# Moving the work beside each attention one stage on: gates beside stick-breaking, the triangular solve beside forgetting attention, the recurrence beside differential attention

## The chip, the cores and the metric

The kernel runs on one core of one Trainium2 chip. The core has a matrix engine (TensorE, PE in the views; its weight loads are listed apart as PEld), VectorE (DVE), ScalarE (ACT), GpSimd (POOL) and SyncE (SP, which issues most transfers). Each engine executes its own instructions in a fixed order; semaphores tie the engines together. The metric is the device time of one execution in microseconds, lower is better.

## The reference

One layer of a hybrid encoder for 1024 prompt tokens and 64 tokens of a second request with 256 cached positions (1088 rows in all, `D_MODEL` 1024). Four branches read one projection of the normalized input, and each has a gate of 1024 columns:

```python
u = rms_norm(x);  proj = u @ w_in          # fox | diff | sb | gdn | gates (4 x 1024)
o_fox  = softmax(q k^T/8 + c_q - c_k) v    # forgetting attention, 4 heads of 64
o_diff = (softmax_1 - lam * softmax_2) v   # differential attention, then a norm
z = q k^T/8                                # stick-breaking attention
o_sb   = exp(log_sigmoid(z) + later) v     # later: reversed cumsum of log_sigmoid(-z)
# gated DeltaNet, chunks of 64 tokens, 4 heads of 64
sol = triangular_solve(I + m, [v*beta, k*beta*exp(g)])   # per chunk and head
for each chunk:
    v_new = u - kc @ S
    o = (q*exp(g)) @ S + a @ v_new
    S = S*exp(g_last) + k'^T @ v_new
merged = sum_i sigmoid(gate_i) * (o_i @ w_branch_i)
x += merged @ w_out;  x += swiglu(rms_norm(x));  y = rms_norm(x)
```

## The kernel before

Matrices are split into a high and a low float16 half, and each product is three matmuls. The program goes through stages, one after the other: norm and transposes; the DeltaNet projection (`gdn_project`); `gdn_pass1`, which works out per chunk the 64x64 matrices m (stored through the dram tile `nd`), decays and scaled keys (`r1d`, `r2d`, `qed`); then the three attentions `attend_sb`, `attend_fox`, `attend_diff`; the merge; the product with `w_out` (tile `pout`); the feed-forward part.

Each attention loops over two pairs of heads and nine query tiles (`QORD`). Per tile TensorE makes scores into `psc`, VectorE and ScalarE turn them into probabilities in `st` (for stick-breaking: `z`, `e` and a reversed scan `cu`), a transposing transfer brings `st` back as `pt`, and TensorE multiplies by the values into `pv` (`po` in the differential attention).

Two lists hold work that is written beside these stages. `dense` is TensorE work: the projections of the three attentions (`project`, tile `pd`, stored to `qd_*`, `kd_*`, `vd_*`) and the gates (`spill_gates`): for each branch, 8 column tiles of 128 and 3 pieces of the 1088 rows, 96 tiles of 24 matmuls into `pgs`, each copied by ScalarE into `ths` and stored to `gtd` by a POOL-issued transfer. `side` is the DeltaNet's serial part: `gdn_solve` (30 steps of the triangular solve on VectorE, tiles `X` and `tmpx`, all chunks and heads at once) and `gdn_seq` (the recurrence over the row tiles t = 8, 0, 1 to 7; two chunks each but for t = 8). A step of `gdn_seq` prepares `py`, `px`, `pu`, `pk`, and then per chunk:

```python
pks = kc @ (Sh, Sl);  vn = u0 - pks;  vh = split(vn)
pds = kd @ vh;  pog = qe @ (Sh, Sl) + aa @ vh
S32 = S1 + pds;  Sh, Sl = split(S32)
```

After its chunks, a row tile gets its norm (`sqo`, `sso`, `ztg`, `osg`) and is stored to `od_gdn`. `fill(us)` takes as much from `dense` as the constants `FILL_SB`, `FILL_FOX`, `FILL_DIFF`, `FILL_GDN` allow, and one piece of `side`. A scheduler then fixes each engine's order from the instructions so written, from their data and from the pools that they need. `drain` writes the rest of a list.

What stands beside what: beside `gdn_pass1` and `attend_sb`, the projections; `gdn_solve` beside `attend_sb` (its first step is held behind `sb_mark`); beside `attend_fox` the recurrence and the gates, which reach through `attend_diff`. The merge takes the branches in the order sb, fox, diff, gdn (tile `ptb`, 96 tiles): its pool `brp`, with `oT` (the branch outputs, transposed) and the branch weights `wbh`, `wbl`, is opened after the recurrence's pool is closed. A gate tile comes back from `gtd` as `thg`; its tanh is on ScalarE, the product and the sum `mg` on VectorE, some sums on POOL.

Of the kernel before, what the change touches and what calls it, by code (L numbers as in the profile page):

```python
# [44 lines left out]

FILL_SB, FILL_FOX, FILL_DIFF, FILL_GDN = 0.0143, 0.006, 0.0155, 8

# [6 lines left out]
def tile_hybrid_encoder(ctx, tc, i, o):  # L54
# [461 lines left out]

    sb_mark = [None]

    def attend_sb():
        for pair in range(2):  # L520
            kT, vt = load_kv("sb", pair)
            for t in QORD:
# [3 lines left out]
                for hp in range(2):  # L526
# [19 lines left out]
                    acopy(sv[:n, 0, :W], z[:n, :W], PS)  # L546
                    sb_mark[0] = stt(sv[:n, 1, :W], z[:n, :W], PS, sv[:n, 0, :W], ALU.mult, ALU.subtract)
                    pts.append(tr())
# [3 lines left out]
    def attend_fox():  # L552
        for pair in range(2):
# [4 lines left out]
            for t in QORD:  # L558
# [3 lines left out]
                for hp in range(2):  # L562
# [15 lines left out]
                    acopy(sv[:n, 0, :W], s[:n, :W], mn[:n, 3:4])  # L578
                    stt(sv[:n, 1, :W], s[:n, :W], mn[:n, 3:4], sv[:n, 0, :W], ALU.mult, ALU.subtract)
                    pts.append(tr())  # L580
# [115 lines left out]
    qed = tc.dram_tile([T, 512], F16, name="qed")  # L696
    nd = tc.dram_tile([18, NH, 64, 64], F32, name="nd")
    xd = tc.dram_tile([17 * NH, 2048], F32, name="xd")
# [5 lines left out]
    def gdn_pass1(g1p, xg):  # L704
# [54 lines left out]
        def scores_of(t, n, gt, rec2):  # L759

            pm = pgd("pm")
            for c in range(1 if t == 8 else 2):
                for h in range(NH):
                    for xy in range(2):
                        pe.matmul(pm[64 * c:64 * c + 64, h * P:(h + 1) * P],
                                  lhsT=gt[:, 2 + xy, h, 64 * c:64 * c + 64],
                                  rhs=gt[:, 0:2, h, 64 * c:64 * c + 64], start=(xy == 0), stop=(xy == 1))
            pm4 = pm.rearrange("p (h v i) -> p h v i", h=NH, v=2)
            dt_t = dT[:, t * NH:(t + 1) * NH]
            a32 = g1p.tile([P, NH, 64], F32, tag="a32", name="a32", bufs=1)  # L770
            n32 = g1p.tile([P, NH, 64], F32, tag="n32", name="n32", bufs=2)
            stt(n32[:n], pm4[:n, :, 1], -(2.0 ** -10), dt_t[:n], ALU.mult, ALU.mult)
            stt(a32[:n], pm4[:n, :, 0], 2.0 ** -5, dt_t[:n], ALU.mult, ALU.mult)
            ra = rec2[:, 1024:].rearrange("p (l h e) -> p l h e", l=2, h=NH)
            acopy(ra[:n, 0], a32[:n])
            tt(ra[:n, 1], a32[:n], ra[:n, 0], ALU.subtract)
            sync.dma_start(r2d[t, 0:n], rec2[:n])
            for c in range(1 if t == 8 else 2):
                gps.dma_start(nd[2 * t + c].rearrange("h j i -> j h i"), n32[64 * c:64 * c + 64])

# [81 lines left out]
    def gdn_solve():  # L862
# [3 lines left out]
        with tc.tile_pool(name="gp2", bufs=1, side="right", reuse_waits="tile") as g2p:  # L866
            X = g2p.tile([NP, 2, 32, 32], F32, name="X")
            tmp = g2p.tile([NP, 512], F32, name="tmpx")
            for q in range(2):
                sl = slice(32 * q, 32 * q + 32)  # L870
                gps.dma_start(X[:, q], nd[0:17, :, sl, sl].rearrange("n h j i -> (n h) j i"))
            for _ in range(3):
                yield 0.0
            for j in range(1, 31):
                r = 31 - j
                behind = tc.issue_after(sb_mark[0].ins) if j == 1 else ExitStack()
                behind.__enter__()
# [18 lines left out]
    def gdn_seq(g3):  # L896
# [30 lines left out]
        for t in [8] + list(range(8)):  # L927
# [11 lines left out]
            for c in range(nch):  # L939
                up, dn = slice(64 * c, 64 * c + 32), slice(64 * c + 32, 64 * c + 64)  # L940
                sync.dma_start(t32[up, :, 0:32], xv[2 * t + c, 0])
                sync.dma_start(t32[dn, :, 32:64], xv[2 * t + c, 1])
                sync.dma_start(t32[up, :, 32:64], nd[2 * t + c, :, 0:32, 32:64].rearrange("h j i -> j h i"))
                sync.dma_start(t11[64 * c:64 * c + 32], xtv[2 * t + c])
# [98 lines left out]

    def spill_gates(b, sp):
        j = bidx[b]
        for d2 in range(4):
            wu = load_unit([(w_in, 0, OFF_GATE + j * D + d2 * BW, BW)], BW)
            for m in range(2):
                d = 2 * d2 + m
                for off, n in PIECES:  # L1050
                    pg = pd("pgs")
                    gemm_a(pg, wu, m * P, uh, ul, off, n, KD)
                    th = sp.tile([P, 364], F32, tag="ths", name="ths", bufs=2)
                    with tc.high_priority():
                        acopy(th[:, :n], pg[:, :n], 0.5 * IWS)
                    gps.dma_start(gtd[b][d * P:(d + 1) * P, off:off + n], th[:, :n])
                    yield 3.7


    with tc.tile_pool(name="gp1", bufs=1, side="right", reuse_waits="tile") as g1p:  # L1060
# [8 lines left out]
        proj = [project(b) for b in ("sb", "fox", "diff")]  # L1069
        dense += proj  # L1070
        for w in gdn_pass1(g1p, xg):
# [7 lines left out]
    with tc.issue_after(pre.ins):  # L1079
        side.append(gdn_solve())  # L1080
        attend_sb()
    drain(dense)
    drain(side)
    pj_.close()
    cb_ = ExitStack()
    cb = cb_.enter_context(tc.tile_pool(name="cb", bufs=1, side="right", reuse_waits="tile"))
    gd_ = ExitStack()
    g3 = gd_.enter_context(tc.tile_pool(name="gp3", bufs=1, side="right", reuse_waits="tile"))
    dense += [spill_gates(b, sp) for b in gtd]
    side.append(gdn_seq(g3))  # L1090
    attend_fox()
    drain(side)
    gd_.close()
    cb_.close()
    br_ = ExitStack()
    brp = br_.enter_context(tc.tile_pool(name="br", bufs=1, side="right", reuse_waits="tile"))
    attend_diff()
    drain(dense)
# [411 lines left out]
```

## Time and profile before

| | |
|---|---|
| time, 3 runs | median 1852.74 us (1850.4 to 1865.82) |
| the profiled execution: own time / span | 1846.53 / 1844.7 us |
| TensorE busy / weight loads busy | 1731.3 us (94%) / 1226.5 us (66%) |
| VectorE / ScalarE / GpSimd busy | 1253.2 / 864.1 / 302.9 us |
| first scores of sb, fox, diff | 301 / 492 / 641 us |
| last gate matmul, first `pout` matmul | 957 / 1065 us |

The stages are told apart by the first matmul of each tile name. Times in the views are microseconds from the start of the span, where not marked ns. A busy share is an average over the whole span; the stretches between these marks have different limits, so the rows below are cut by them.

### The profile page before, as it was taken

To read this page: it belongs to the slowest core of one execution; us is meant where nothing else is said; L and a number is where in the kernel's file an instruction comes from. 1 tells how busy PE (TensorE), PEld (TensorE's weight loads), DVE (VectorE), ACT (ScalarE), POOL (GpSimd) and SP (SyncE) were. 2 spreads that over 40 slices of the span, in tenths; PEclk is the share of its full clock that TensorE was granted. 3 is DMA by queue.
4 is the path that set the end of the run, shared out by engine and by line. 5 is a ranking of instruction groups with operands and counts; after the bars stand their busy time and mean duration, and the time that the engine had idled before them with its cause. 6 is when DMAs were issued, how large, how long until landed. Compare 5 with 4: busy or idle time off the path is not lost.

```text
span 1844.7 us, 36720 instructions
## 1 busy us (share of the span) xinstructions
PE 1731.3 (94%) x14364; PEld 1226.5 (66%) x14364; DVE 1253.2 (68%) x2589; ACT 864.1 (47%) x1819; POOL 302.9 (16%) x445
## 2 busy tenths in 40 slices
PE   7999887798898899999998899999999999999997
PEld 5678775675565566666565588777758668577573
DVE  7558874899766576877757886757546456465455
ACT  6335555888755554655646533423314224132132
POOL 2113221001222222232334620000000000000002
PEclk9999998899999999999999999999999999999999
DMA  6267689989899975664949746412212112112113
GB/s 227 50 107 200 209 245 167 217 185 208 181 193 214 191 154 143 147 163 102 251 133 285 209 132 108 101 52 58 70 35 78 37 48 81 35 35 69 35 47 103
DMA packets 412157, 244.60 MB, mean 133 GB/s; under 512 B 266146, under 2 KB 389502, under 8 KB 411916
## 3 DMA queue, kind: packets, MB, share of 16 engines
q1 hardware_dynamic: 398944, 205.67, 47.1%
q0 software_dynamic: 13040, 36.60, 7.4%
q8 instruction: 112, 1.84, 0.4%
q14 instruction: 61, 0.50, 0.1%
HBM read 123.39 MB, written 60.81 MB: 100 GB/s over the span
## 4 chain that ended last, share of the span: by engine, by line
PE 66%; DMA 13%; DVE 11%; issue 5%; ACT 3%; POOL 1%; SPq 1%; DVEq 0%; POOLq 0%; ACTq 0%
PE po L1432 12%; PE pgs L185 5%; PE pgs L183 5%; PE pgs L184 5%; DMA pt<-st 4%; PE pb L1316 3%; PE pb L1315 3%; PE pb L1317 3%; PE pc L1316 2%; PE pc L1317 2%; PE pa L1317 2%; PE pc L1315 2%; PE pa L1316 2%; PE pa L1315 2%; PE psc L456 2%
## 5 line engine op out<-in xcount | busy, mean ns | idle before, releaser
L183 PE MATMUL pgs<-u,wh 128*128 128x364 f16 (+1 forms) x768 | 245.3, 319 | 2.7 <-ACT ths L61 2.7
L185 PE MATMUL pgs<-u,wl 128*128 128x364 f16 (+1 forms) x768 | 245.5, 320 | 0.0
L184 PE MATMUL pgs<-u,wh 128*128 128x364 f16 (+1 forms) x768 | 245.4, 320 | 0.0
L1432 PE MATMUL po<-wh,hT 128*128 128x512 f16 (+1 forms) x792 | 238.1, 380 | 0.6 <-DVE x2a L64 0.6
L1432 PEld LDWEIGHTS <-hT 128*128 128x128 f16 (+1 forms) x1188 | 109.2, 99 | 120.0 <-issue 7.6
L64 DVE SCALAR_TENSOR_TENSOR x2a<-po,x2a 128x512 f32<-128x512 f32 x108 | 74.5, 690 | 140.2 <-PE po L1432 140.0
L61 ACT ACTIVATE wh<-w32f 128x1024 f16<-128x1024 f32 (+1 forms) x90 | 80.3, 926 | 160.6 <-PE po L1432 111.7
L1315 PE MATMUL pb<-X,wh 128*128 128x288 f16 (+1 forms) x528 | 147.1, 279 | 2.5 <-DMA X<-nsh 2.2
L64 DVE SCALAR_TENSOR_TENSOR wl<-w32f,wh 128x1024 f16<-128x1024 f32 (+1 forms) x90 | 94.7, 1066 | 79.8 <-ACT wh L61 79.7
L1316 PE MATMUL pb<-X,wh 128*128 128x288 f16 (+1 forms) x528 | 147.2, 279 | 0.3 <-DMA X<-nsl 0.3
L1317 PE MATMUL pb<-X,wl 128*128 128x256 f16 (+1 forms) x528 | 146.3, 279 | 0.0
L1432 PE MATMUL po<-wl,hT 128*128 128x512 f16 (+1 forms) x396 | 142.0, 379 | 0.0
L1315 PEld LDWEIGHTS <-wh 128*128 128x128 f16 x1232 | 120.5, 98 | 31.0 <-issue 2.3
L1316 PEld LDWEIGHTS <-wh 128*128 128x128 f16 x1232 | 120.5, 98 | 30.0 <-issue 2.4
L1317 PEld LDWEIGHTS <-wl 128*128 128x128 f16 x1232 | 120.5, 98 | 27.2 <-issue 0.9
L165 PE MATMUL pd<-wh,u 128*128 128x256 f16 (+1 forms) x448 | 125.6, 280 | 4.0 <-DVE qs L64 2.6
L167 PE MATMUL pd<-wh,u 128*128 128x256 f16 (+1 forms) x448 | 125.0, 279 | 0.0
L166 PE MATMUL pd<-wl,u 128*128 128x256 f16 (+1 forms) x448 | 125.0, 279 | 0.0
L184 PEld LDWEIGHTS <-wh 128*128 128x128 f16 x912 | 89.8, 98 | 51.9 <-issue 4.1
L185 PEld LDWEIGHTS <-wl 128*128 128x128 f16 x912 | 89.6, 98 | 51.0 <-issue 2.6
L183 PEld LDWEIGHTS <-wh 128*128 128x128 f16 x912 | 89.7, 98 | 50.4 <-issue 1.5
L71 POOL TENSOR_SCALAR fss<-fss 128x1 f32<-128x1 f32 (+1 forms) x9 | 2.0, 219 | 660.3 <-ACT fsq L1461 660.3
(393 smaller groups left out, 4642.7 us busy)
## 6 DMA issues: line engine op xcount, KB each, us to landing
w<-in_w_in_dram SPq DMA_DIRECT2D x56, 512.0 KB, 4.8
w32f<-in_w_ffn_gate_dram SPq DMA_DIRECT2D x20, 512.0 KB, 5.0
w32f<-in_w_ffn_up_dram SPq DMA_DIRECT2D x20, 512.0 KB, 4.0
w32f<-in_w_ffn_down_dram SPq DMA_DIRECT2D x20, 512.0 KB, 4.0
xt<-in_x_prompt_dram SPq DMA_DIRECT2D x8, 512.0 KB, 6.8
wb<-in_w_branch_dram SPq DMA_DIRECT2D x8, 512.0 KB, 4.8
w<-in_w_out_dram SPq DMA_DIRECT2D x8, 512.0 KB, 5.8
x2a<-in_x_prompt_dram SPq DMA_DIRECT2D x8, 512.0 KB, 6.7
```

The source lines that it names most:

```text
L61: return act.activation(out, in_, AF.Copy, scale=scale)
L64: return vec.scalar_tensor_tensor(out=out, in0=in0, scalar=s, in1=in1, op0=op0, op1=op1)
L165: pe.matmul(ps[:n, :N], lhsT=a, rhs=wh[:, k, :N], start=(k == 0), stop=False)
L166: pe.matmul(ps[:n, :N], lhsT=a, rhs=wl[:, k, :N], start=False, stop=False)
L167: pe.matmul(ps[:n, :N], lhsT=b, rhs=wh[:, k, :N], start=False, stop=(k == K - 1))
L183: pe.matmul(ps[:, :n], lhsT=a, rhs=xh[:, k, off:off + n], start=(k == 0), stop=False)
L184: pe.matmul(ps[:, :n], lhsT=a, rhs=xl[:, k, off:off + n], start=False, stop=False)
L185: mm = pe.matmul(ps[:, :n], lhsT=b, rhs=xh[:, k, off:off + n], start=False, stop=(k == K - 1))
L1315: pe.matmul(ps[:, :n], lhsT=wh[:, k], rhs=xh_, start=(start and k == 0), stop=False, skip_group_check=not start)
L1316: pe.matmul(ps[:, :n], lhsT=wh[:, k], rhs=xl_, start=False, stop=False, skip_group_check=not start)
L1317: mm = pe.matmul(ps[:, :n], lhsT=wl[:, k], rhs=xh_, start=False, stop=(k == 3), skip_group_check=not start)
L1432: pe.matmul(ps[h * n:h * n + n], lhsT=hts[k + h][:, a, tk:tk + n], rhs=w[:, k + h], start=(k == 0 and a == 0 and w is wh), stop=(k + nh >= ...
```

## The change

`gdn_pass1` has only the sb and fox projections beside it. Each branch's gates become four generators of six tiles (`spill_gates(b, sp, d2)`), put on `dense` ahead of `attend_sb`, behind what is left of the fox projection. Then `attend_fox` has the diff projection and `gdn_solve` beside it (held behind a mark in `attend_fox`), and `attend_diff` has the recurrence and the rest of the gates. `brp` is opened when the recurrence and `attend_diff` have been written, and `dense` is drained after that. `FILL_FOX` is 0.0085 in place of 0.006. `nd` holds three 32x32 blocks per matrix: each of the 17 stores becomes three, the load of `X` one transfer in place of two. No matmul, VectorE or ScalarE instruction is added or taken away.

```diff
-FILL_SB, FILL_FOX, FILL_DIFF, FILL_GDN = 0.0143, 0.006, 0.0155, 8
+FILL_SB, FILL_FOX, FILL_DIFF, FILL_GDN = 0.0143, 0.0085, 0.0155, 8
...
-    nd = tc.dram_tile([18, NH, 64, 64], F32, name="nd")
+    nd = tc.dram_tile([18, NH, 3, 32, 32], F32, name="nd")
...
-                gps.dma_start(nd[2 * t + c].rearrange("h j i -> j h i"), n32[64 * c:64 * c + 64])
+                for b, (j0, i0) in enumerate(((0, 0), (32, 32), (0, 32))):
+                    gps.dma_start(nd[2 * t + c, :, b].rearrange("h j i -> j h i"),
+                                  n32[64 * c + j0:64 * c + j0 + 32, :, i0:i0 + 32])
...
-            for q in range(2):
-                sl = slice(32 * q, 32 * q + 32)
-                gps.dma_start(X[:, q], nd[0:17, :, sl, sl].rearrange("n h j i -> (n h) j i"))
+            gps.dma_start(X.rearrange("p b j i -> p b (j i)"), nd[0:17, :, 0:2].rearrange("n h b j i -> (n h) b (j i)"))
...
-        dense += proj
+        dense += proj[0:2]
...
     with tc.issue_after(pre.ins):
-        side.append(gdn_solve())
+        dense += [spill_gates(b, sp, d2) for b in gtd for d2 in range(4)]
         attend_sb()
-    drain(dense)
-    drain(side)
-    pj_.close()
+    drain(dense, proj[1])
+    drain(dense, dense[0])
     cb_ = ExitStack()
     cb = cb_.enter_context(tc.tile_pool(name="cb", bufs=1, side="right", reuse_waits="tile"))
+    dense.insert(0, proj[2])
+    side.append(gdn_solve())
+    attend_fox()
+    drain(dense, proj[2])
+    drain(side)
+    cb_.close()
+    pj_.close()
     gd_ = ExitStack()
     g3 = gd_.enter_context(tc.tile_pool(name="gp3", bufs=1, side="right", reuse_waits="tile"))
-    dense += [spill_gates(b, sp) for b in gtd]
     side.append(gdn_seq(g3))
-    attend_fox()
+    attend_diff()
     drain(side)
     gd_.close()
-    cb_.close()
     br_ = ExitStack()
     brp = br_.enter_context(tc.tile_pool(name="br", bufs=1, side="right", reuse_waits="tile"))
-    attend_diff()
     drain(dense)
```

**Place 1, TensorE, the last matmuls ahead of the first product of the merge (`ptb`).** Before; `pgs` are gates:

```order
L184 LDWEIGHTS wh
L184 MATMUL pgs<-u_103,wh 128x364
L185 LDWEIGHTS wl
L185 MATMUL pgs<-u_103,wl 128x364
L183 LDWEIGHTS wbh
L183 MATMUL ptb<-oT,wbh 128x364
```

After, first where the last gate stands, then where the first `ptb` stands, some 670 rows further on; `pds` and `pog` belong to the recurrence:

```order
L184 LDWEIGHTS wh
L184 MATMUL pgs<-u_103,wh 128x360
L185 LDWEIGHTS wl
L185 MATMUL pgs<-u_103,wl 128x360
L1011 LDWEIGHTS rec2b
L1011 MATMUL pds<-vh_8779,rec2b 128x64
```

```order
L1017 LDWEIGHTS rec2b
L1017 MATMUL pog<-vh_8781,rec2b 64x64
L1018 LDWEIGHTS rec2b
L1018 MATMUL pog<-vh_8781,rec2b 64x64
L183 LDWEIGHTS wbh
L183 MATMUL ptb<-oT,wbh 128x364
```

Before, gates stand on both sides of the first `ptb` (459 gate matmuls come behind the last chunk of the recurrence). After, the last gate stands ahead of the `pds` of t = 5's second chunk; the last remainders of `attend_diff`, then t = 6 and t = 7 alone, fill the rows up to the first `ptb`.

**Place 2, TensorE, the rows ahead of the first score of `attend_sb` (`psc`).** Before, with `pd` the projections:

```order
L166 LDWEIGHTS u_103
L166 MATMUL pd<-wl,u_103 128x256
L167 LDWEIGHTS u_103
L167 MATMUL pd<-wh,u_103 128x256
L456 LDWEIGHTS qt
L456 MATMUL psc<-kT,qt 128x512
```

After:

```order
L183 LDWEIGHTS wh
L183 MATMUL pgs<-u_103,wh 128x360
L184 LDWEIGHTS wh
L184 MATMUL pgs<-u_103,wh 128x360
L456 LDWEIGHTS qt
L456 MATMUL psc<-kT,qt 128x512
```

The projections ahead of the first score have given way to gates; 143 gate matmuls stand ahead of it after, none before, and 48 projection matmuls fewer.

**Place 3, VectorE, the middle of `attend_sb`.** Before, `X` and `tmpx` being the solve:

```order
L67 TENSOR_TENSOR X<-X,tmpx 68x2x19x12
L64 SCALAR_TENSOR_TENSOR st<-z,st 128x1024
L67 TENSOR_TENSOR z<-z,cu 128x896
L71 TENSOR_SCALAR cu<-z 128x896
L67 TENSOR_TENSOR tmpx<-X 68x440
L541 SCALAR_TENSOR_TENSOR cu<-cu,e 128x896
L67 TENSOR_TENSOR X<-X,tmpx 68x2x20x11
L67 TENSOR_TENSOR z<-z,cu 128x896
```

After:

```order
L541 SCALAR_TENSOR_TENSOR cu<-cu,e 128x896
L67 TENSOR_TENSOR z<-z,cu 128x896
L71 TENSOR_SCALAR cu<-z 128x896
L64 SCALAR_TENSOR_TENSOR st<-z,st 128x1024
L64 SCALAR_TENSOR_TENSOR os<-pv,os 128x128
L64 SCALAR_TENSOR_TENSOR wl<-w_6050,wh 128x1024
L64 SCALAR_TENSOR_TENSOR wl<-w_6054,wh 128x1024
L541 SCALAR_TENSOR_TENSOR cu<-cu,e 128x896
```

The solve's steps, which stood between the `cu`, `z` and `st` rows of the attention, have gone; all 60 stand in `attend_fox` after.

## Rows read from the trace of the kernel before

**Rows 1.** The page: busy time, share of the span and instructions of each engine.

```profile
PE 1731.3 (94%) x14364; PEld 1226.5 (66%) x14364; DVE 1253.2 (68%) x2589; ACT 864.1 (47%) x1819; POOL 302.9 (16%) x445
```

**Rows 2.** The span cut at the marks of the table: stretch, its length, then busy us (and instructions) of each engine, the granted TensorE clock as a share of full speed, the busy share of the 16 DMA engines, GB/s. The stretches are: all before `attend_sb`; the sb stretch; the fox stretch; the diff stretch; the last gates with the first `ptb`; the rest of the merge; the rest of the program; a piece of the feed-forward part.

```profile
0.00:302.00 302.00, 267.11 (x2274) 214.98 (x2275) 205.59 (x386) 147.78 (x300) 70.30 (x108) 0.97 0.70 171
302.00:492.00 190.00, 166.47 (x1542) 118.04 (x1540) 167.36 (x297) 158.06 (x314) 25.01 (x37) 0.94 0.95 200
492.00:641.00 149.00, 132.56 (x1475) 85.67 (x1474) 95.63 (x305) 82.83 (x189) 31.93 (x52) 0.95 0.98 196
641.00:895.00 254.00, 251.01 (x2336) 164.91 (x2334) 187.31 (x560) 140.04 (x363) 72.44 (x114) 1.00 0.64 153
895.00:957.00 62.00, 59.32 (x439) 37.73 (x437) 41.93 (x147) 35.53 (x99) 16.76 (x29) 1.00 0.65 161
957.00:1065.00 108.00, 90.76 (x563) 54.73 (x560) 85.89 (x142) 60.97 (x122) 57.03 (x54) 0.98 0.79 233
1065.00:1845.00 780.00, 764.09 (x5749) 550.46 (x5748) 469.48 (x755) 238.94 (x432) 29.44 (x52) 0.99 0.24 66
1315.00:1500.00 185.00, 185.00 (x1265) 120.97 (x1263) 98.91 (x162) 44.99 (x81) 0.00 (x0) 1.00 0.16 46
```

**Rows 3.** What TensorE waited for in the sb stretch (with the wait that ends at its first score): us in total, times, longest.

```profile
PE pv L468 <- DMA pt<-st: 16.8, 5, 6.7
PE psc L456 <- DMA qt<-qd_sb: 9.9, 1, 9.9
```

**Rows 4.** The same of the fox stretch.

```profile
PE pv L468 <- DMA pt<-st: 7.6, 6, 2.8
PE psc L456 <- DMA qt<-qd_fox: 5.8, 2, 3.5
```

**Rows 5.** The same of the rest of the merge.

```profile
PE ptb L183 <- DVE thg L64: 12.3, 13, 1.8
```

**Rows 6.** SyncE's queue ahead of the first score of `attend_sb`: start, us, the transfer issued.

```profile
280.40 3.59 SPq L480 DMA_TRANSPOSE kT<-kd_sb  x1
...
287.68 1.26 SPq L491 DMA_TRANSPOSE qt<-qd_sb  x1
...
289.84 6.25 SPq L491 DMA_TRANSPOSE qt<-qd_sb  x2
```

**Rows 7.** TensorE's first score of `attend_sb`, with the idle time before it in brackets.

```profile
301.43 0.61 PE L456 MATMUL psc<-kT,qt 128*128 128x512 f16 x1 [9.88 <-DMA qt<-qd_sb]
```

**Rows 8.** TensorE, two matmuls of a gate tile, one after the other, at full clock: start, us.

```profile
901.18 0.32 PE L183 MATMUL pgs<-u,wh 128*128 128x360 f16 x1
901.34 0.32 PE L184 MATMUL pgs<-u,wh 128*128 128x360 f16 x1
```

**Rows 9.** The stores of `nd` in `gdn_pass1`, issued by POOL: count, busy us of the issue, mean ns.

```profile
L779 POOL DMA_DIRECT2D nd<-n x17 | 11.1, 656 | 11.3 <-DVE n L64 11.0 <-issue 0.2
```

**Rows 10.** VectorE in the sb stretch by groups: count, busy us, mean ns of one, idle time before them. `X` and `tmpx` are the solve's; `ks` and `qs` the projections' (the low half of keys and queries).

```profile
L67 DVE TENSOR_TENSOR X<-X,tmpx 68x60 f32<-68x60 f32 (+14 forms) x30 | 14.6, 488 | 0.1
L67 DVE TENSOR_TENSOR tmpx<-X 68x60 f32<-68x60 f32 (+14 forms) x30 | 14.5, 482 | 0.1
...
L64 DVE SCALAR_TENSOR_TENSOR ks<-e,ks 128x256 f16<-128x256 f32 (+1 forms) x18 | 6.8, 415 | 0.0
L64 DVE SCALAR_TENSOR_TENSOR qs<-pd,qs 128x256 f16<-128x256 f32 (+1 forms) x14 | 5.3, 417 | 5.1 <-ACT qs L61 5.1
```

**Rows 11.** Transfers issued in the sb stretch: count, KB each, median us from issue to landing.

```profile
kd_diff<-ks SPq DMA_DIRECT2D x10, 256.0 KB, 3.0
qd_diff<-qs SPq DMA_DIRECT2D x8, 256.0 KB, 2.9
gtd_sb<-ths POOLq DMA_DIRECT2D x10, 182.0 KB, 4.5
```

**Rows 12.** VectorE, the recurrence's last chunk (`vn`, `vh`, `S32p`) and the norm of its last row tile: start, us, idle before in brackets.

```profile
869.23 0.43 DVE L64 SCALAR_TENSOR_TENSOR vn<-pks,u 64x256 f32<-64x256 f32 x1 [0.33 <-PE pks L999]
...
870.13 0.42 DVE L67 TENSOR_TENSOR vh<-vn,vh 64x256 f16<-64x256 f32 x1 [0.29 <-ACT vh L61]
...
874.14 0.42 DVE L64 SCALAR_TENSOR_TENSOR S32p<-pds,S 128x256 f32<-128x256 f32 x1 [0.83 <-PE pds L1011]
...
876.20 0.41 DVE L1032 TENSOR_REDUCE sso<-sqo 128x4 f32<-128x256 f32 x1
...
880.40 0.42 DVE L67 TENSOR_TENSOR ztg<-ztg,pog 128x256 f32<-128x256 f32 x1
...
881.30 0.43 DVE L67 TENSOR_TENSOR osg<-ztg,osg 128x256 f16<-128x256 f32 x1 [0.22 <-ACT osg L61]
```

**Rows 13.** POOL over the same time: the two small steps of the norm, the last store of `od_gdn`, the first load of `oT`.

```profile
876.71 1.16 POOL L72 TENSOR_SCALAR sso<-sso 128x4 f32<-128x4 f32 x1 [1.19 <-DVE sm L67]
877.95 1.96 POOL L67 TENSOR_TENSOR sso<-sso,mhb 128x4 f32<-128x4 f32 x1
...
882.02 0.54 POOL L1040 DMA_DIRECT2D od_gdn<-osg  x1 [0.97 <-DVE osg L67]
...
884.39 0.79 POOL L1126 DMA_DIRECT2D oT<-od_sb  x1 [0.66 <-DMA thg<-gtd_sb]
```

**Rows 14.** The first loads of `oT`: count, KB each, median us from issue to landing.

```profile
oT<-od_sb POOLq DMA_DIRECT2D x2, 544.0 KB, 5.8
```

**Rows 15.** VectorE from 895 us to the end of the merge, the sums of its first branch (sb): count, busy us, mean ns, idle before.

```profile
L64 DVE SCALAR_TENSOR_TENSOR mg<-thg,ptb 128x364 f32<-128x364 f32 (+1 forms) x24 | 12.2, 530 | 11.1 <-ACT thg L1145 10.5 <-PE ptb L185 0.5
```

More of the change, by code (lines that the diff above doesn't have):

```diff
@@ L515, in fill @@
             side.pop(0)
-    sb_mark = [None]
+    at_mark = [None]
     def attend_sb():
@@ L546, in attend_sb @@
                     acopy(sv[:n, 0, :W], z[:n, :W], PS)
-                    sb_mark[0] = stt(sv[:n, 1, :W], z[:n, :W], PS, sv[:n, 0, :W], ALU.mult, ALU.subtract)
+                    stt(sv[:n, 1, :W], z[:n, :W], PS, sv[:n, 0, :W], ALU.mult, ALU.subtract)
                     pts.append(tr())
@@ L578, in attend_fox @@
                     acopy(sv[:n, 0, :W], s[:n, :W], mn[:n, 3:4])
-                    stt(sv[:n, 1, :W], s[:n, :W], mn[:n, 3:4], sv[:n, 0, :W], ALU.mult, ALU.subtract)
+                    at_mark[0] = stt(sv[:n, 1, :W], s[:n, :W], mn[:n, 3:4], sv[:n, 0, :W], ALU.mult, ALU.subtract)
                     pts.append(tr())
@@ L875, in gdn_solve @@
                 r = 31 - j
-                behind = tc.issue_after(sb_mark[0].ins) if j == 1 else ExitStack()
+                behind = tc.issue_after(at_mark[0].ins) if j == 1 else ExitStack()
                 behind.__enter__()
@@ L942, in gdn_seq @@
                 sync.dma_start(t32[dn, :, 32:64], xv[2 * t + c, 1])
-                sync.dma_start(t32[up, :, 32:64], nd[2 * t + c, :, 0:32, 32:64].rearrange("h j i -> j h i"))
+                sync.dma_start(t32[up, :, 32:64], nd[2 * t + c, :, 2].rearrange("h j i -> j h i"))
                 sync.dma_start(t11[64 * c:64 * c + 32], xtv[2 * t + c])
@@ L1042, in tile_hybrid_encoder, with spill_gates @@
     bidx = {"fox": 0, "diff": 1, "sb": 2, "gdn": 3}
-    def spill_gates(b, sp):
+    def spill_gates(b, sp, d2):
         j = bidx[b]
[L1046 to L1057, printed above, removed]
+        wu = load_unit([(w_in, 0, OFF_GATE + j * D + d2 * BW, BW)], BW)
+        for m in range(2):
+            d = 2 * d2 + m
+            for off, n in PIECES:
+                pg = pd("pgs")
+                gemm_a(pg, wu, m * P, uh, ul, off, n, KD)
+                th = sp.tile([P, 364], F32, tag="ths", name="ths", bufs=2)
+                with tc.high_priority():
+                    acopy(th[:, :n], pg[:, :n], 0.5 * IWS)
+                gps.dma_start(gtd[b][d * P:(d + 1) * P, off:off + n], th[:, :n])
+                yield 3.7
     with tc.tile_pool(name="gp1", bufs=1, side="right", reuse_waits="tile") as g1p:
```

## The prediction, made before the changed kernel ran

> **What bounds the kernel now.** The page comes first: TensorE is busy for 1731 of 1845 us [rows 1], so only what it loses can be won, since the change adds and removes no matmul. The table by stretches says where it loses. In the piece of the feed-forward part it is busy for 185.00 of 185 us, in the diff stretch for 251.01 of 254 [rows 2]: nothing can be gained there. The losses lie in three places. The sb stretch has 190 us with 166.5 busy, and its clock is granted at 0.94: 23.5 us idle and about 190 x 0.06 = 11 us of slow clock, 35 lost. The fox stretch has 149 with 132.6 busy at 0.95: 16.4 idle and 7.5 of clock, 24 lost. The rest of the merge has 108 with 90.8 busy, 17 lost [rows 2]. The waits of TensorE name what it lacked: in the sb stretch the transposed probabilities `pt`, 16.8 us, and the first queries, 9.9 us, which end at the first score [rows 3]; in the fox stretch `pt` 7.6 and queries 5.8 [rows 4]; in the merge the slots of the gate tiles, 12.3 [rows 5].
>
> Behind the waits for `pt` in the sb stretch stand three candidates: VectorE, busy 167 of 190 us, ScalarE 158, and the transfer engines at 95% [rows 2]. In the fox stretch the first two are far from full (96 and 83 of 149) and the transfers are at 98%. In the diff stretch the transfers are at 64% and TensorE waits for nothing. So the two attentions with projections beside them lose time, the one with gates beside it doesn't.
>
> I make the sum of TensorE's losses against the profiled execution, 1846.5 us of its own time. The runs lie 4 to 19 us above it (median 1852.7); I leave that difference to the range. A change of 1% (18.5 us) is about what a measurement of this kernel can tell from none.
>
> **Start of the sb stretch.** Before, keys and queries come through transposing loads in SyncE's queue, the last pair issued from 289.84 to 296.1 [rows 6], and the first score comes after 9.88 us of idle [rows 7], in which TensorE has nothing else to do. In the new order 143 gate matmuls stand ahead of that score. At one per 0.15 to 0.16 us [rows 8] they are 22 us of work, brought forward, enough to cover the idle time. But more stands ahead of those key loads on SyncE: two loads of cached keys, two of weights and a key store of the diff projection. And `gdn_pass1` gets longer on POOL: 51 stores in place of 17, at 656 ns each [rows 9], are 22 us more of issuing, between which its other small steps have to pass. POOL was busy for 70 of these 302 us [rows 2], which hides it; without that cover up to 22 us would come to the end of the pass, but then the gates stand ready to fill. I take **-5**, from -10 (all of the idle gone) to +5.
>
> **The sb stretch.** The solve leaves it, 60 VectorE instructions and 14.6 + 14.5 = 29 us, and with the diff projection go the low halves of keys, queries and values, 12.1 us for `ks` and `qs` alone [rows 10]. VectorE falls from 167 to some 120 us; ScalarE loses only the copies and gets the gates' instead, about 145 of what were 158. TensorE keeps its amount, with gates in place of projections: 148 before and 143 after by counts and step times of the rows. The stores of the diff projection (ten and eight of 256 KB [rows 11] and the smaller ones) leave, gate stores of 182 KB come. So two of the three candidates are relieved, the third a little. I expect the waits for `pt` to halve (-8), the remaining idle time (23.5 - 16.8 = 6.7) to shrink by 5 and the slow clock, which came with the idle time, by 7: **-20**. The bounds are 0 (transfers were the cause and stay so) and -35 (nothing is lost); ScalarE's 145 us keep the stretch at 150 or longer.
>
> **The fox stretch.** It receives what the sb stretch gave: 60 solve instructions, the diff projection with its low halves and stores. It gives away two steps of the recurrence and most of its gates. VectorE goes from 96 to about 96 + 29 + 16 less 20 for the recurrence = 121 of 149, still with room. The diff projection's stores are about 8 MB (18 of 256 KB [rows 11], 10 values of half that and the outputs of both); 16 gate tiles of 182 KB and seven recurrence loads of 384 KB, 5.6 MB, leave. At this stretch's 196 GB/s [rows 2] the net 2.4 MB are some 13 us of a resource that is at 98%. Against it, the step of TensorE's own work there rises only from 113 to 120 us, and a gate tile, which waited for ScalarE, is gone. I take **0**; the bounds are -24 (no loss is left) and +20 (13 of transfers, and 7 for solve steps standing ahead of `st` on VectorE). The load of `X` stands far from its use and costs nothing.
>
> **The diff stretch.** It now has the whole recurrence beside gates, 272 us of TensorE work in place of 236. Beside gates it ran without loss before (251 of 254); **+1**, from 0 to 10.
>
> **The end of the recurrence.** This is the new wait. Before, 459 gate matmuls stood behind the recurrence's last chunk, and the stretch from 895 to 957 lost 62 - 59.3 = 2.7 us [rows 2]. In the new order the last gate stands ahead of the end of t = 5 (place 1 of the change), and the first `ptb` can't start before the last row tile is normed: `oT` and the branch weights live in a pool that is opened when the recurrence's is closed, and on POOL the first `oT` load stands behind the last `od_gdn`. So TensorE waits through a chain. One chunk alone: four VectorE steps at 0.42 (`vn`, `vh`, `S32p` are shown [rows 12], `Sl` is like `vh`), two ScalarE halves that fit in the 0.47 between `vn` and `vh`, some 0.4 of small matmuls and six hand-overs at 0.3 (the brackets show 0.29 and 0.33): 1.7 + 0.9 + 0.4 + 1.8 = 4.8 us. A row tile is two of them and some 4.3 for `py` to `kc`: 13.9 for t = 7. Of t = 6, whose preparation lies beside the last diff tiles, 7.7 remain. The rest of t = 5 and the last diff tiles are VectorE's: 127 instructions stand from the last gate to the branch weights' low halves, 42 us by the durations of like rows, 28 of them ahead of t = 6. The norm takes from 876.2 to 881.7 with its square ahead, 6.3 [rows 12, 13]; POOL then issues `od_gdn` (0.54) and two `oT` loads (0.79 each), which land in 5.8 [rows 13, 14], 8 together. The sum is 28 + 7.7 + 13.9 + 6.3 + 8 = 64 us, in which TensorE has 14 us of work: 50 lost against 2.7, **+47**. The bounds: VectorE's 42 us back to back and the loads, less 14, are +34; with the 28 stretched by VectorE's share of such a stretch (41.9 of 62 [rows 2]) it is +60.
>
> **The merge.** It lost 12.3 us to gate slots in its first branch, whose 24 tiles [rows 15] before stood partly among gates. Now none does. At 12.3 / 20, some 0.6 us a tile, four more tiles wait: **+3**, from 0 to 12.
>
> **Sum.** -5 - 20 + 0 + 1 + 47 + 3 = +26: 1846.5 + 26 = 1872 us.
>
> **Rivals.** *The sb stretch runs to its floor.* If VectorE alone caused its losses, it gives 35 and not 20, and the start 10 and not 5: 1872 - 20 = 1852. For it speaks that VectorE is the fullest engine there after TensorE; against it, the fox stretch lost nearly as much of its length (24 of 149, against 35 of 190) with VectorE at 64%. *The fox stretch inherits the trouble* (slower still): transfers are its limit at 98% and the diff projection adds 13 us of them, with 7 for the solve: 1872 + 20 = 1892. It decides if the fox stretch is longer than 160 us. *Faster than before:* no attention loses anything, because it was projection beside stick-breaking that made the losses: -35, -10 and -24 in the fox stretch with the end at +45: about 1826. That needs more than 50 us of gain ahead of the diff stretch, to outweigh the exposed end; the diff projection in the fox stretch speaks against it. *The diff stretch has room.* By its weight loads TensorE is busy for 164.9 of 254 us there, 65%, and for 550.5 of 780, 71%, in the rest of the program [rows 2]; at that share the same work would fit into 254 x 65 / 71 = 233 us, and the chain of the recurrence would come forward by 21: 1851. Against this stand two rows: the piece of the feed-forward part has 121 of 185, 65% too, with TensorE busy throughout, and the gates alone have 37.7 of 62, 61%. So the share tells which shape of matmul runs, not how much room there is. The rule behind this rival is in the Trainium skill, "Perfetto Trace Analysis", section "Identifying the Most-Contended Engine": the busy share of matmuls misleads, that of weight loads is the better measure. This trace doesn't bear it out for these shapes.
>
> **How the numbers follow.** The forecast has 0.44, the floor of the sb stretch 0.22, the fox stretch's trouble 0.19, faster 0.10, room in the diff stretch 0.05. A tenth of the whole, the lower edge of the forecast's own range of 1860 to 1885, lies within 1% of 1852.7, with the two rivals at 1852: same 0.10 + 0.22 + 0.05 = 0.37. Slower is the rest of the forecast and the fox rival, 0.34 + 0.19 = 0.53; faster 0.10. The range of 8 in 10 leaves out the faster case and the worst of the fox case: 1840 to 1900.
>
> **What would show it.** After the change the stretch ahead of the first `psc` of sb has no idle of 10 us; the sb stretch is some 170 us long with `pt` waits near 8; the fox stretch about 150. Between the last `pgs` and the first `ptb` there are some 64 us in which TensorE is busy for less than 20, and no gates stand in the merge. The forecast is wrong if that stretch is shorter than 45 us, or if the two attentions lose over 20 us less, or more, than said.

## The result and the profile after

The changed kernel takes 1866.9 us against 1852.7 before (medians of 20 runs each); the ratio is 1.0062, with a 95% interval of 1.0039 to 1.0085: 11.5 us slower, within 1%. (Three of the changed kernel's runs, at 1873.6 to 1874.0 us, count as slow and are left out of the ratio, so it isn't quite that of the medians.) The forecast was 1872, from 1840 to 1900. The profiled execution took 1856.4 us, with a span of 1854.7, 10 more than before; it lies 10 us below its median, the one of before 6 below.

The page's busy times, which answer to [rows 1], say little: the work is the same.

```profile
PE 1740.3 (94%) x14364; PEld 1236.0 (67%) x14364; DVE 1251.0 (67%) x2589; ACT 866.6 (47%) x1819; POOL 307.1 (17%) x478
```

The span cut at the same marks as [rows 2] (stretch, length, busy us of PE, PEld, DVE, ACT, POOL, granted clock, DMA share, GB/s). The fifth line is new: from the last gate matmul to the first product of the merge, `ptb`.

```profile
0.00:314.70 314.70, 287.14 (x2371) 225.07 (x2372) 206.52 (x386) 150.44 (x306) 86.96 (x149) 0.97 0.72 178
314.70:473.40 158.70, 149.88 (x1312) 94.36 (x1311) 122.17 (x174) 144.32 (x289) 28.75 (x46) 1.00 0.83 174
473.40:619.30 145.90, 132.30 (x1368) 100.23 (x1367) 113.70 (x348) 85.88 (x184) 18.98 (x30) 0.95 0.99 216
619.30:901.40 282.10, 278.03 (x2599) 182.62 (x2598) 214.24 (x663) 158.67 (x418) 73.25 (x123) 0.99 0.66 154
901.40:961.30 59.90, 30.36 (x398) 24.35 (x395) 37.26 (x123) 28.36 (x80) 18.08 (x30) 0.56 0.33 97
961.30:1076.10 114.80, 96.96 (x576) 58.11 (x575) 87.72 (x142) 60.23 (x114) 52.17 (x50) 0.95 0.79 244
1076.10:1854.70 778.60, 765.62 (x5749) 551.27 (x5748) 469.40 (x755) 238.70 (x432) 28.91 (x52) 1.00 0.24 67
```

TensorE's loss in a stretch is its idle time and what a slower clock costs its busy time, busy x (1 - clock). In us:

| stretch | before | after | difference | forecast |
|---|---|---|---|---|
| ahead of the first sb score | 42.9 | 36.2 | -7 | -5 |
| sb | 33.5 | 8.8 | -25 | -20 |
| fox | 23.1 | 20.2 | -3 | 0 |
| diff | 3.0 | 6.9 | +4 | +1 |
| end of the recurrence (before: last gates) | 2.7 | 42.9 | +40 | +47 |
| merge | 19.1 | 22.7 | +4 | +3 |
| rest of the program, in pieces of 20 us | 17.4 | 15.7 | -2 | 0 |

The sums of the two columns differ by 12, and the span grew by 10. The clock has two digits, which is up to 1.5 us in each of the first six rows. In the last stretch, with 765 us of busy time, a hundredth of clock would be 8 us; so its row is added up from pieces of 20 us. It executes the same instructions in both and is 780 and 779 us long.

What TensorE waited for, which answers to [rows 3, 4]: from 250 us to the first sb score, in the sb stretch, and in the fox stretch.

```profile
PE pgs L183 <- ACT ths L61: 5.6, 2, 3.9
```

```profile
PE pv L468 <- DMA pt<-st: 5.8, 6, 1.7
```

```profile
PE pv L468 <- DMA pt<-st: 7.6, 7, 2.7
PE pv L468 <- DVE os L64: 5.8, 1, 5.8
PE psc L456 <- DMA qt<-qd_fox: 0.2, 1, 0.2
```

The waits for `pt` in the sb stretch went from 16.8 to 5.8 us, and the clock is full. The wait of 9.9 us for the first queries is gone; in its place TensorE waits 5.6 us for ScalarE to empty gate tiles into `ths`. Now the exposed end. What TensorE waited for most between last gate and first `ptb`, and six of its rows there (start, us, idle before in brackets):

```profile
PE ptb L183 <- DMA oT<-od_sb: 11.0, 1, 11.0
PE pds L1011 <- ACT vh L61: 4.1, 5, 1.0
```

```profile
920.76 0.29 PE L977 MATMUL pu<-rec1b,ttbd 128*128 128x64 f16 x2 [1.32 <-ACT ttbd L61]
...
933.07 0.63 PE L951 MATMUL py<-t,tt 32*32 32x32 f32 x8
...
942.15 0.26 PE L998 MATMUL pks<-Sh,kc 128*64 128x64 f16 x1 [1.42 <-DVE kc L67]
...
943.80 0.21 PE L1011 MATMUL pds<-vh,rec2b 128*128 128x64 f16 x1 [1.01 <-ACT vh L61]
...
950.05 0.24 PE L1018 MATMUL pog<-vh,rec2b 128*64 128x64 f16 x1
...
961.30 0.46 PE L183 MATMUL ptb<-oT,wbh 128*128 128x364 f16 x1 [11.01 <-DMA oT<-od_sb]
```

The first `pu` of t = 6 starts at 920.76, the first `py` of t = 7 at 933.07, its first chunk at 942.15, and its last small matmul ends at 950.3. The hand-overs of the chain can be seen: about 1 us before a `pds`, for a half of `vh`, and 11.0 us for `oT`. Between them TensorE does small matmuls at a granted clock of 0.56, mostly the lower of its two levels. The first `ptb`, of 364 columns, takes 0.46 us, where a gate matmul of 360 columns takes 0.32 at full clock [rows 8]. POOL shows why `oT` comes last:

```profile
956.37 0.62 POOL L1040 DMA_DIRECT2D od_gdn<-osg  x1 [2.20 <-DVE osg L67]
957.18 1.47 POOL L1128 DMA_DIRECT2D oT<-od_sb  x2 [0.20 <-issue]
```

The loads are issued after the last store of `od_gdn`, as its order said. ScalarE adds a small delay that the forecast didn't have, a table load and three `thg` of the merge in front of the state's half `Sh`, for which VectorE then waits 0.77 us:

```profile
930.86 1.28 ACT L1147 ACT_TABLE_LOAD   x1
932.15 1.30 ACT L1147 ACTIVATE thg<-thg 128x364 f32<-128x364 f32 x3
933.36 0.40 ACT L61 ACTIVATE Sh<-S32p 128x256 f16<-128x256 f32 x1
```

```profile
933.79 0.42 DVE L64 SCALAR_TENSOR_TENSOR Sl<-S32p,Sh 128x256 f16<-128x256 f32 x1 [0.77 <-ACT Sh L61]
```

### The profile page after: what moved, and what is told of

The parts are those of the page before. It is cut to its first block, busy times and chain, and to the rows that moved or that the text cites. A ratio compares the mean times of both kernels' runs of the same rounds, so it can differ in the third digit from the quotient of the medians.

```text
span 1854.7 us, 36819 instructions
## 1 busy us (share of the span) xinstructions
PE 1740.3 (94%) x14364; PEld 1236.0 (67%) x14364; DVE 1251.0 (67%) x2589; ACT 866.6 (47%) x1819; POOL 307.1 (17%) x478
## 4 chain that ended last, share of the span: by engine, by line
PE 58%; DVE 6%; DMA 6%; ACT 2%; issue 1%; POOL 0%; SPq 0%; DVEq 0%; POOLq 0%; ACTq 0%
PE po L1434 12%; PE pgs L183 4%; PE pgs L185 4%; PE pgs L184 4%; DMA pt<-st 3%; PE pb L1317 3%; PE pb L1318 3%; PE pb L1319 3%; PE pa L1319 2%; PE pc L1318 2%; PE pa L1318 2%; PE pa L1317 2%; PE pc L1319 2%; PE pc L1317 2%; PE pout L165 1%
```

## The experiments

**What the exposed end costs.** Both kernels were run without the last two row tiles of the recurrence.

```diff
-        for t in [8] + list(range(8)):
+        for t in [8] + list(range(6)):
...
+            for t_ in (5, 6, 7) if t == 5 else (t,):
+                gps.dma_start(od["gdn"][t_ * P:t_ * P + n], os_[:n].rearrange("p l c -> p (l c)"))
```

> The changed kernel without the recurrence's last two row tiles (t = 6 and 7 are left out, the rows of t = 5 are stored in their place); everything ahead of t = 6 stands as it was. Theory A (the recurrence's end is exposed: no gate is left behind t = 5): the time between the last gate and the first product of the merge falls from 60 to some 35 to 42 us and the whole gets 18 to 25 us faster than the changed kernel, though only 8 us of TensorE work are gone. Rival C (the end is not what TensorE waits for; loads of the merge are): the gain is the 8 us of work or less.

> The kernel before without the recurrence's last two row tiles, as the control: 459 gate matmuls stand behind its last chunk. Theory A (there the recurrence is covered): the gain is the 8 us of TensorE work that are gone, 5 to 11 us. Rival C: as much as in the changed kernel without them.

Measured: the changed kernel without them takes 0.9845 (0.9791 to 0.9900) of the kernel before, 1823 us; with them 1.0062. That is some 40 us for two row tiles. The control takes 0.9936 (0.9910 to 0.9962), 11 us less for the same work. So about 29 us of the two tiles' cost is exposure, give or take some 12 by the intervals. The changed kernel's end stretch without them, from the last gate to the first `ptb`:

```profile
915.60:936.10 20.50, 5.85 (x80) 4.22 (x79) 16.26 (x67) 14.44 (x42) 12.76 (x21) 0.71 0.46 128
```

It is 20.5 us long in place of 59.9. Rival C is out. The gain is larger than Theory A's 18 to 25, and the stretch shorter than its 35 to 42. One reason is in the rows above: from the first `pu` of t = 6 to the last small matmul of t = 7 the chain takes 29.5 us, where the forecast had 7.7 + 13.9 for these two. The other 10 us of the shorter stretch weren't separated; some 46 matmuls that stood behind the last gate also moved ahead of it (398 - 80, less the 272 of the two row tiles).

**Solve or projection?** One of the two moves was undone in each: first the solve is beside `attend_sb` again, then the diff projection, ahead of the gates.

```diff
+        side.append(gdn_solve())
         attend_sb()
...
-    side.append(gdn_solve())
     attend_fox()
```

```diff
+        dense.append(proj[2])
         dense += [spill_gates(b, sp, d2) for b in gtd for d2 in range(4)]
...
-    dense.insert(0, proj[2])
```

> The changed kernel with one part undone: the triangular solve stands beside the stick-breaking attention again, the diff projection stays beside the forgetting attention, the recurrence beside the differential attention. In the changed kernel the stick-breaking stretch lost 9 us of idle time and nothing of clock (159 us, clock 1.00), before it lost 35 of 190. Theory A (VectorE, relieved of the solve, gave that gain): the stretch loses 20 to 35 us again and is 172 to 187 us long, the forgetting stretch gets 5 to 10 us shorter, and the whole is 5 to 20 us slower than the changed kernel. Rival B (the projection's small-packet stores and its half-clock spells made the loss): the stretch stays within 5 us of 159, the whole within 8 us of the changed kernel.

> The changed kernel with another part undone: the projections of the differential attention stand beside stick-breaking again (456 projection matmuls and 432 gate matmuls in it, 721 gate matmuls in the changed kernel), the solve stays beside the forgetting attention. Theory A (the solve on VectorE): the stick-breaking stretch keeps most of its gain, with under 15 us of idle time and clock lost, some 155 to 165 us for 134 us of TensorE work. Rival B (the projection's transfers): idle time and clock lost are 25 us or more there, and the forgetting stretch loses 10 us less than the 20 of the changed kernel.

Measured: 1.0112 (1.0061 to 1.0163) with the solve back, 1.0085 (1.0047 to 1.0123) with the projection back. Their sb stretches, in this order:

```profile
314.30:483.60 169.30, 157.94 (x1337) 98.56 (x1336) 145.72 (x238) 147.85 (x290) 31.47 (x52) 0.98 0.81 176
```

```profile
340.90:508.80 167.90, 158.55 (x1462) 109.93 (x1461) 133.24 (x204) 152.96 (x311) 19.81 (x32) 0.97 0.86 192
```

Each is some 10 us longer than the changed kernel's 158.7, with 5 to 6 us more lost (idle and clock) and 8 us more of busy time, and far from the 190 of before. Rival B fails in both: the solve alone was to leave the stretch within 5 us of 159, the projection alone to bring 25 us of loss or more. Theory A fails with the solve back, which was to bring 20 to 35 us of loss; with the projection back its loss of under 15 us holds (14), its length of 155 to 165 is missed by 3. So neither piece of work alone is the cause. In the second kernel the profiled execution lost another 29 us ahead of the first score, where TensorE waited for the low half of a query tile on VectorE. At 1885.1 us it is the slowest of the ten runs (median 1865.2), so this profile isn't a typical run of that kernel.

**The layout alone.** The four edits of `nd` were put into the kernel before.

> The kernel before with only the layout of the 64x64 matrices changed (51 stores in place of 17, one load of X in place of two). By the prediction the stores are hidden behind POOL's idle time: within 4 us of the kernel before; if POOL's longer queue held up the end of the first pass, the first score of stick-breaking would come up to 22 us later.

Measured: 0.9937 (0.9912 to 0.9962), 1841.6 against 1854.3 us. This is a gain of 12 us, which the prediction had priced at nothing. So it was repeated, and the opposite was run on the same chip: the changed kernel with the old layout.

> The kernel before with only the new layout, once more with five rounds: 0.3 to 0.9% faster than before if the first result holds; within 0.2% if it was scatter.

> The changed kernel once more, on one chip with the three runs that follow, so that they can be compared: 0.4 to 0.9% slower than before.

> The changed kernel with the old layout of the 64x64 matrices (17 stores, two loads of X). The kernel before with the new layout alone was 0.6% faster than before, which nobody expected. Theory F (the layout itself is worth 8 to 14 us, and the moved stages cost 20 to 25): 1.2 to 1.6% slower than before, 10 us slower than the changed kernel; it should show as DMA time, since the old load of X moves 128-byte pieces beside the stick-breaking attention. Rival G (that gain belonged to the other instruction order that the edit brought about, or to the first pass): within 5 us of the changed kernel, where the load of X stands far from its use.

Measured: the layout alone 0.9937 again (0.9911 to 0.9962); the changed kernel 1.0059 (1.0034 to 1.0083); with the old layout 1.0151 (1.0117 to 1.0185), 1882 against 1864 us. Theory F's ratio holds and Rival G's number fails: the layout is worth 0.6% in one kernel and 0.9% in the other, and the moved stages by themselves cost 1.5%, some 28 us. The sb stretch of the changed kernel with the old layout:

```profile
305.20:496.90 191.70, 167.44 (x1399) 103.28 (x1398) 124.54 (x181) 149.37 (x296) 34.00 (x54) 0.94 0.83 165
```

It is 191.7 us long, with 24 us idle and the clock at 0.94, though neither solve nor diff projection stands in it and VectorE is busy for only 125 us. In the two profiles of the layout alone, where both stand in it, the stretch is shorter:

```profile
314.30:499.80 185.50, 163.57 (x1479) 113.21 (x1478) 159.88 (x276) 153.95 (x306) 23.38 (x38) 0.95 0.85 188
```

```profile
302.40:482.40 180.00, 161.09 (x1479) 112.06 (x1478) 159.99 (x278) 153.95 (x306) 23.31 (x38) 0.96 0.87 195
```

What happens at the start of the changed kernel's sb stretch with the old layout is seen on POOL, ScalarE and TensorE (start, us, idle before), in the loads' landing time, and in the stretch's first two pieces of 20 us:

```profile
287.44 3.17 POOL L871 DMA_DIRECT2D X<-nd  x1 [1.08 <-PE pd L167]
304.22 3.10 POOL L871 DMA_DIRECT2D X<-nd  x1 [13.61 <-issue]
307.31 1.19 POOL L1055 DMA_DIRECT2D gtd_sb<-ths  x2
```

```profile
X<-nd POOLq DMA_DIRECT2D x2, 272.0 KB, 19.2
```

```profile
326.80 0.47 ACT L61 ACTIVATE ths<-pgs 128x360 f32<-128x360 f32 x1 [18.86 <-DMA gtd_sb<-ths]
```

```profile
327.33 0.46 PE L183 MATMUL pgs<-u,wh 128*128 128x364 f16 x1 [14.88 <-ACT ths L61]
```

```profile
305.00:325.00 20.00, 7.45 (x36) 3.88 (x35) 1.47 (x1) 2.66 (x4) 3.50 (x3) 0.68 1.17 140
325.00:345.00 20.00, 16.66 (x90) 9.50 (x90) 12.65 (x13) 17.60 (x25) 2.17 (x4) 0.81 0.81 166
```

The old `X` is two loads of 128-byte pieces, 68 x 32 each. POOL needs 3.1 us to issue one, waits 13.6 us before it can issue the second, and they land in 19.2 us. The next gate stores stand behind them in POOL's queue. ScalarE waits 18.9 us for the first of these to free a slot of `ths`, and TensorE 14.9 us for ScalarE. Added up from pieces of 20 us, the stretch loses 31 us, and 21 of them lie in these first 40, at the wait and the slower clock around it. The other 152 lose 10, about what the changed kernel loses in its whole sb stretch. With the new layout `X` is one load of 8 KB pieces, 0.56 us to issue, and the gate store follows at once:

```profile
293.13 0.56 POOL L871 DMA_DIRECT2D X<-nd  x1 [0.30 <-issue]
293.69 0.57 POOL L1055 DMA_DIRECT2D gtd_sb<-ths  x1
```

```profile
301.81 0.47 ACT L61 ACTIVATE ths<-pgs 128x360 f32<-128x360 f32 x1 [10.23 <-DMA gtd_sb<-ths]
```

There, too, ScalarE waits for the stores behind it, three times and 19.4 us in all, and the load lands after 16.3 us; but only 5.6 us of it reach TensorE, ahead of the first score.

In the kernel before no gate store stands behind the two loads. POOL's next issue after them is a store of `od_sb`, and that one waits for VectorE:

```profile
306.14 3.09 POOL L871 DMA_DIRECT2D X<-nd  x1 [18.16 <-issue]
342.61 0.71 POOL L473 DMA_DIRECT2D od_sb<-os  x1 [33.38 <-DVE os L64]
```

So the wait in POOL's queue can explain what the layout is worth in the changed kernel, in one profile, but not the 12 us that the layout alone gives. Their cause stays open; the edit also changes the instruction order elsewhere.

**Can the recurrence get more cover?** Three kernels with gates kept back: the first has the first line of this diff alone, the second all of it, the third the last lines alone, with t = 5 in place of 4.

```diff
-FILL_SB, FILL_FOX, FILL_DIFF, FILL_GDN = 0.0143, 0.0085, 0.0155, 8
+FILL_SB, FILL_FOX, FILL_DIFF, FILL_GDN = 0.0095, 0.0085, 0.0155, 8
...
+                seq_mark[t] = acopy(vh[sl, 0], vn[sl])
...
-    drain(dense)
+    with tc.issue_after(seq_mark[4].ins):
+        drain(dense)
```

> The changed kernel with FILL_SB 0.0095 in place of 0.0143: 880 gate matmuls stand ahead of the recurrence's first chunk in place of 1125, so some ten gate tiles more are left for the recurrence, and the last gate stands in t = 7 in place of t = 5. Theory A (the gates are the recurrence's cover; a row tile uses up some seven of them, and what is left of the chain when they are gone is lost): the time between the last gate and the first product of the merge falls from 60 to 25 to 35 us, the stick-breaking stretch keeps its 160 us, and the whole is 20 to 35 us faster than the changed kernel, 10 to 25 faster than before. Rival D (the stick-breaking stretch needs the gates: it loses what the end gains): within 8 us of the changed kernel.

> As the kernel with FILL_SB 0.0095, and the gates that are left when the differential attention has been written wait for the first ScalarE half of t = 4: some 25 tiles stand beside t = 4 to 7 and the last gate behind the norm's first steps, while t = 4's first part stands without gates. Theory A: the end from the last gate to the first product of the merge shrinks to 10 to 20 us, but 10 to 20 us are lost at t = 4; the whole lies within 8 us of the kernel without the hold. Rival D: as for that kernel.

> The changed kernel with the same gates in the stick-breaking stretch, but the 12 tiles that are left when the differential attention has been written wait for the first ScalarE half of t = 5. Theory A (the number of gates beside the recurrence counts, not their place): t = 4 and the first of t = 5 lose what the end wins; the whole lies within 10 us of the changed kernel. Rival E (only the end is dear, since the merge's loads are exposed there too): 15 to 30 us faster than the changed kernel.

Measured: 1.0092 (1.0062 to 1.0123), 1.0140 (1.0098 to 1.0182), 1.0052 (1.0021 to 1.0083). With the lower constant the end shrinks as forecast, to 30 us, but the forecast gain of 20 to 35 us doesn't come. Its sb, fox and end stretches, and one wait of TensorE in fox:

```profile
324.00:478.90 154.90, 142.05 (x1367) 99.19 (x1366) 128.93 (x194) 146.49 (x286) 22.12 (x34) 1.00 0.85 185
478.90:606.40 127.50, 104.18 (x1037) 72.49 (x1036) 99.58 (x324) 73.08 (x169) 15.52 (x25) 0.87 0.93 194
952.10:982.50 30.40, 9.96 (x139) 8.06 (x137) 12.85 (x27) 15.20 (x32) 7.87 (x12) 0.59 0.24 79
```

```profile
PE psc L456 <- DMA qt<-qd_fox: 10.9, 6, 3.6
```

The fox stretch now has 104 us of busy TensorE in 127.5 and a clock of 0.87; it waits for queries and loses 17 us more than the changed kernel's, the end 18 less. Gates aren't what it lacks, it has 142 gate matmuls in place of 129. But where gates were kept back from sb, 361 matmuls of the diff projection moved up into it, and fox has 287 of them left in place of 648. Rival D was right on the sum and wrong on the place (fox, not sb).

With the gates held behind t = 5, the diff stretch and the end are:

```profile
620.80:943.50 322.70, 303.29 (x2889) 200.71 (x2888) 242.01 (x769) 173.97 (x471) 89.16 (x145) 0.95 0.63 149
943.50:966.00 22.50, 7.05 (x108) 6.00 (x105) 9.27 (x16) 12.76 (x25) 5.94 (x9) 0.59 0.20 63
```

The end loses 18 us in place of 43, the diff stretch 35 in place of 7, and the whole changes by nothing measurable against 1.0059 to 1.0062. Theory A holds, and Rival E is out. Holding them behind t = 4 with the lower constant brings the end to 15.9 us, within its forecast, and the whole is slower by 0.5%, with intervals that overlap. So a shorter end alone wins nothing: what it gains is lost in the diff stretch when the gates are held, and in fox with the lower constant.

**VectorE relieved without moving a stage.** The layout alone, and the solve's steps on POOL, the products in the same way as the sums shown.

```diff
-                tt(X[:, :, 0:j, j + 1:32], X[:, :, 0:j, j + 1:32], tj, ALU.add)
+                tt(X[:, :, 0:j, j + 1:32], X[:, :, 0:j, j + 1:32], tj, ALU.add, eng=gps)
```

> The kernel before with the new layout and with the 60 steps of the triangular solve on POOL in place of VectorE, still beside stick-breaking; nothing else is moved, so the recurrence keeps its place and its cover. Theory A (VectorE's 29 us of solve make the losses of the stick-breaking stretch): the stretch loses under 25 us in place of 35 and is 165 to 178 us long, the end stays covered, and the whole is 10 to 25 us faster than before. Rival H (POOL needs twice the time or more for a step, and od_sb and gate stores queue behind it; or both engines slow each other): the stretch gains nothing and the whole is at the time of the layout alone or slower.

Measured: 1.0092 (1.0057 to 1.0127), so Rival H holds. Its sb stretch, POOL's steps in it (count, busy us, mean ns), a row of VectorE while they run and the same row later, and a group of VectorE:

```profile
310.30:521.90 211.60, 172.34 (x1584) 117.28 (x1583) 171.07 (x238) 157.71 (x317) 91.52 (x90) 0.91 0.77 177
```

```profile
L67 POOL TENSOR_TENSOR X<-X,tmpx 68x300 f32<-68x300 f32 (+14 forms) x25 | 36.5, 1459 | 1.9
L67 POOL TENSOR_TENSOR tmpx<-X 68x336 f32<-68x336 f32 (+14 forms) x24 | 30.8, 1284 | 1.8
```

```profile
319.68 1.85 DVE L67 TENSOR_TENSOR z<-z,cu 128x1024 f32<-128x1024 f32 x1
...
443.25 1.22 DVE L67 TENSOR_TENSOR z<-z,cu 128x1024 f32<-128x1024 f32 x1
```

```profile
L64 DVE SCALAR_TENSOR_TENSOR ks<-e,ks 128x256 f16<-128x256 f32 (+1 forms) x18 | 16.5, 958 | 0.1
```

A step takes 1.28 to 1.46 us on POOL in place of 0.49 on VectorE [rows 10]. VectorE's own rows become slower beside them: POOL's steps run until 384 us, and the same `z` of 1024 columns takes 1.85 us among them and 1.22 behind them; the mean `ks` takes 0.96 us, 0.42 before [rows 10]. The stretch is 212 us long. VectorE is busy for 171 us in it, more than the 160 of the layout alone, so it wasn't relieved, and this run doesn't test Theory A.

## Why the prediction was right or wrong

**Sign, range and main mechanism: right.** The end of the recurrence is exposed as worked out: 59.9 us, where 64 were forecast. TensorE is busy for 30 of them, not for less than 20 as the forecast's sign had it, because the clock is near half; at full clock this is some 17, where 14 were forecast. The loss is 43, 40 more than before; the term was 47. By part, in the chain of waits: the rest of t = 5 with the last diff tiles, up to the first `pu` of t = 6 at 920.8, took 19.4 us (28 forecast). From there to `py` of t = 7 it took 12.3 (7.7 forecast). Then `py` to the first chunk of t = 7 took 9.1 (4.3 forecast) and its two chunks 8.1 (9.6). The norm and the loads took 11.0 (14.3 forecast). ScalarE's table load is not what lengthened the middle: it cost one wait of 0.77 us. The parts miss by up to 9 us, and their sum is near because the errors cancel, which is luck.

**Start, -5: measured -7, but not settled.** Three kernels with the same order ahead of the first score (the changed one, and the two with the lower constant) reached it at 314.7, 324.0 and 309.9 us. A single profile can't tell 5 us there.

**The sb stretch, -20: near in size (-25) and in its parts.** The waits for `pt` fell by 11 us (8 forecast), the other idle time by 4 (5 forecast), the slow clock by 10 (7 forecast). Which of the two things moved out brought this, the prediction left open ("two of the three candidates are relieved"), and the runs don't single one out: with the new layout the stretch loses 25 to 30 us when both stand in it, 14 when either is moved out and 9 when both are. With the old layout it loses 34 in either kernel, but for different reasons: in the changed order two thirds of it are the wait behind the loads of `X` and the slower clock around that wait.

**The layout: the step that was sized at nothing.** The prediction gave the new `nd` only its cost, the 34 added stores on POOL, and for the rest it says: "The load of `X` stands far from its use and costs nothing." In the changed kernel this is nearly so, as the gate stores behind the load hold up TensorE for 5.6 us. But the old loads were not free, and what they cost has no term in the sum. The layout is worth 12 us in the kernel before and 17 in the changed one.

**The fox stretch, 0: right** (-3). Taking in the solve and the diff projection cost nothing visible; the rival of 1892 is out, since the stretch is 146 us long. But the premise "the two attentions with projections beside them lose time, the one with gates beside it doesn't" is a misreading. Before, the last projection matmul starts at 409 us, and what stands beside forgetting attention is gates and the recurrence. The stretch's view for the gates' tile `pgs` alone (busy us of TensorE, then of ScalarE):

```profile
492.00:641.00 149.00, 77.58 (x441) 8.28 (x18) 0.95 0.98 196
```

The fox stretch lost 23 us with gates and no projection in it, and 20 with the projection and fewer gates. So the record doesn't support projections as the mark of a stretch that loses.

**The whole.** +26 was forecast against +11.5 measured and +12 in the table. The misses nearly all go the same way: 7 us in the end, 5 in sb, 3 in fox, 2 each at the start and in the rest; only diff and merge go the other way, by 3 and 1. With the old layout the moved stages cost 28 (1.0151), which looks like the forecast, but not by its terms: there sb gives nothing in place of 20, and fox 10 in place of 0. That nearness is luck.

**The rival on the diff stretch** is out: TensorE is busy for 278 of 282 us there, with weight loads at 182.6, 65% as before; 21 us less were needed for that rival. The Trainium skill, "Perfetto Trace Analysis", section "Identifying the Most-Contended Engine", says to judge TensorE's headroom by its weight loads' busy share (and by its arithmetic), not by that of its matmuls. Read in that way, 65% would leave room here; the trace shows 4 us of idle time in 282.

**What beats both** is the layout alone, 0.9937 of the time before in two sets of runs.

## What to carry to other kernels

Work that only fills gaps is a stock: before giving it to one stage, count what the last dependent chain will need, and look at which instructions stand behind the last piece of it. A transfer that is long done before its use may still be dear through the queue in which it is issued: look at who stores through the same queue next. And price an edit that comes along with a move by itself, since here the small one gave back 12 to 17 of the 28 us that the large one lost.

## What was not expected of the hardware

- With the old layout two loads of 272 KB in 128-byte pieces took 3.1 us each to issue, POOL stood 13.6 us between them, and they landed in 19.2 us (median). Of the two gate stores issued behind them from 307.3 on, the first let go of its source at 326.8. The same 544 KB in one load of 8 KB pieces took 0.56 us to issue and 16.3 to land.
- POOL's elementwise steps slowed VectorE's rows beside them: a `z` of 1024 columns took 1.85 us among them and 1.22 behind them, the mean `ks` 958 ns in place of 415.
- In the exposed end the granted clock was 0.54 to 0.56 in every profile that has such an end at full length, after TensorE had been busy almost throughout the 280 us before.
